# Half-precision queries and keys, shifted scan rows, and softmax blocks between stick-breaking blocks

## The chip, the core and the metric

One NeuronCore of a Trainium2 chip runs the whole layer in one launch. The metric is the device time in microseconds (us) of one execution. The engines are TensorE (PE, with its weight loads PEld), VectorE (DVE), ScalarE (ACT), GpSimd (POOL) and SyncE (SP), which here issues the DMAs.

## The reference

One layer on 2048 tokens of width 1024, all in float32:

```python
h = rmsnorm(x, attn_norm_w[l]); proj = h @ w_in[l]        # 1024 -> 3*256 + 3*512 + 3*256
(q_a, k_a, v_a, q_b, k_b, v_b, g_b, g_c, x_c) = jnp.split(proj, split_points, axis=-1)
y_sb = stick_breaking_attention(q_a, k_a, v_a)            # 4 heads of 64
# z = q.k/8;  w[t,s] = sigmoid(z_ts) * prod_{s<j<t} (1 - sigmoid(z_tj)), s < t
qh = rmsnorm(q_b, q_norm_w); kh = rmsnorm(k_b, k_norm_w)
y_ch = chunked_relpos_attention(qh, kh, v_b, rel_bias)    # 8 heads: softmax over a 576-key band + bias
y_cv = g_b * causal_depthwise_conv3(g_c * x_c)
x = x + group_rmsnorm(concat(y_sb, y_ch, y_cv)) @ w_out[l]
x = x + swiglu(rmsnorm(x, ffn_norm_w[l]), w_gate[l], w_up[l], w_down[l])   # d_ff 2816
```

The tokens come to the chip in reverse order, so "nearest keys first" runs along rising columns.

## The kernel before

Every projection takes each operand as a high and a low fp16 part and does three products (`mm3`). Queries and keys are kept as a high and a low part in fp32r (a float32 form that PE takes): `put_parts` writes both parts to DRAM (`kd`, `qd`), and `attend` loads a head's keys as one tile `K` (high part on partitions 0 to 63, low part on 64 to 127) and its queries twice, as `q1` (high, low) and `q2` (low, high). `scores` then needs two products for all four cross terms. A score tile of one block of 128 keys is computed 256 wide (`lead`).

Attention works on tiles of 128 queries. A *stick piece* has up to four blocks of 128 keys. Its `front` computes scores, on ACT two sigmoids (of z into `be`, of -z into `re`), and on DVE a running product of `re` (L609), the product of `be` with the row shifted by one column (L614), and, where an earlier piece of the same tile hands on a carry, a one-column product for column 0 (L612). `re` is a tile for one piece, two buffers. A *softmax piece* (`chunk_tile`) has up to five blocks: scores plus bias with a row maximum on DVE (L646), the negated maximum (L650), Exp with row sum on ACT (L652). In both kinds `mid` transposes the weights on PE, ACT scales and copies them to fp16 (L550), DVE takes the low part (L551); `back` multiplies by the values, and `put_y` writes the result.

The tokens are done in two halves, eight tiles of 128 each; the first half's pieces have few key blocks for the stick heads (1 to 8 a tile), the second's many (9 to 16). `weave` writes PE's order by hand: it takes piece after piece from `attend`, heads 0 to 3 (stick) and then 4 to 11 (softmax), and issues at each step `mid` of the piece three before, `back` of the piece five before and `front` of this one, with a stretch of other PE work between them. That other work is `fill`: the projections of both halves and the first half's output projection. Its steps have costs that add up in `clock` (0.65 for three 512-wide products, 0.33 for three 256-wide ones). How much of it goes between pieces is set by a pace: `origin + at * step - 0.5 * blocks` is what the clock should show after `at` pieces. A head may begin when its projections are `done`, which `later` sets some clock units after them; until then `run` issues fill alone:

```python
for head in range(12):
    need = (half, head // 2 if head < 4 else 2 + (head - 4) // 2)
    while need not in done:
        run(clock[0] + 0.5)
    for p in attend(half, groups, head):
```

On the other engines a planner orders the instructions by the program's order and by when it expects their inputs; each engine then runs its list in order. After the attention and the output projection the FFN of the first half, the second half's output projection and its FFN follow.

Of the kernel before, what the change touches and what calls it, by code (L numbers as in the profile page):

```python
# [9 lines left out]
F32 = mybir.dt.float32  # L10
# [12 lines left out]
NEG = -1e30  # L23
WSC = float(2 ** 14)
# [15 lines left out]
def trunk(ctx: ExitStack, tc: tile.TileContext, x, anw, w_in, qnw, knw, biasx, conv_w, onw, w_out,  # L40
# [18 lines left out]
    xp = ctx.enter_context(tc.tile_pool(name="xp", bufs=6))  # L59
# [12 lines left out]
    nc.gpsimd.affine_select(out=never, in_=never, pattern=[[1, 128]], compare_op=ALU.is_gt, fill=NEG,  # L72
# [4 lines left out]
    cw = consts.tile([128, 2, 3], F32, name="cw")  # L77
    halo = consts.tile([128, 2, 2], F32, name="halo")
# [245 lines left out]
    kd, qd = [{(p, i, j): dp.tile([128, HT], F32R, name=f"{n}d{p}_{i}{j}")  # L324
# [8 lines left out]
    def late_consts():  # L333
        for i, w in enumerate((qnw, knw)):
            for s in range(2):
                nc.sync.dma_start(nw[s * 64:(s + 1) * 64, i:i + 1], w.rearrange("(p o) -> p o", o=1))
        nc.vector.tensor_scalar(nw[:, 0:1], nw[:, 0:1], HD ** -0.5, None, op0=ALU.mult)
        for b in range(2):
            nc.sync.dma_start(cw[:, b, :], conv_w[:, b * 128:(b + 1) * 128].rearrange("t p -> p t"))
# [83 lines left out]
    def put_parts(src, pair, g, d, scale):  # L423

        half, c = where(g)
        hi = ap.tile([128, 520], F32R, name="sth", tag="w2")[:, :GRP]
        lo = ap.tile([128, 520], F32R, name="stl", tag="w2")[:, :GRP]
        nc.scalar.activation(hi, src, AF.Copy, scale=scale)
        nc.vector.scalar_tensor_tensor(lo, src, scale, f32(hi), op0=ALU.mult, op1=ALU.subtract)
        for part, st in enumerate((hi, lo)):  # L430
            nc.sync.dma_start(f32(d[pair, half, part][:, c:c + GRP]), f32(st))
# [23 lines left out]
    def stick_qk(H, groups, W, pair):  # L455
        key = ("qk", pair)
        u = W.get(key)
        for i, d in enumerate((kd, qd)):
            yield from proj_T(H, groups, u[i], lambda g, o, i=i, d=d: put_parts(o, pair, g, d, descale(key, i)))
# [117 lines left out]
    def scores(Q, cols, K, k0, n, diagonal=False):  # L577
# [3 lines left out]
        lead = 128 if n == 128 else 0  # L581
        kc = K[:, k0 - lead:k0 + n]
        nc.tensor.matmul(z[:, :n + lead], q1[:, cols], kc, start=True, stop=False)  # L583
        if diagonal:
            nc.tensor.matmul(z[:, lead:lead + 128], identb, never, start=False, stop=False)
        nc.tensor.matmul(z[:, :n + lead], q2[:, cols], kc, start=False, stop=True)
        return z[:, lead:lead + n]
# [4 lines left out]
    def stick_tile(T, head, K, k0, Q, V, cols):  # L592
# [3 lines left out]
        def piece(b, n):  # L596
# [38 lines left out]
    def chunk_tile(T, head, K, k0, Q, V, cols, bias):  # L635
# [4 lines left out]
        def front():  # L640
# [27 lines left out]
    def attend(half, groups, head):  # L668
# [4 lines left out]
        K = ap.tile([128, HT + more], F32R, name="k", tag="k")  # L673
# [346 lines left out]
```

## Time and profile before

| | |
|---|---|
| median of 3 runs | 2723.12 us (2720.71 to 2726.09) |
| the profiled execution | 2721.8 us, span 2719.9 us, mean granted PE clock 0.978 |
| first half's attention | 99 to 552 us |
| second half's stick heads | 552 to 960 us |
| second half's softmax heads | 960 to 1165 us |
| FFN, with one more output projection | 1288 us to the end |

Busy time is the time in which an engine has an instruction in work. PE's matmuls overlap in their pipeline, so PE can be called busy while its starts are further apart than they could be; the distance between starts is the better measure of one matmul's price.

### The profile page before, as it was taken

The page shows a single profiled execution, that of the slowest core. Times are in us where ns is not written, and L with a number is a line of the kernel's source. Part 1 is how long each engine was busy: PE and PEld are TensorE (multiplying, and loading weights), DVE is VectorE, ACT ScalarE, POOL GpSimd, SP SyncE. Part 2 cuts the span into 40 slices and gives each one's busy share as a digit, 9 for nine tenths or more (in the row PEclk, how much of TensorE's full clock was granted, in tenths as well). Part 3 has the DMA queues.
Part 4 walks back from the last instruction along what each step waited for, and adds up shares of the span by engine and source line. Part 5 has one row for each costly group of instructions (what it writes and reads, how often), then busy time and mean ns, then how long its engine had stood idle before and what let it go on. Part 6 is the DMA issues. An engine that isn't in the chain of part 4 may idle for free.

```text
span 2719.9 us, 41796 instructions
## 1 busy us (share of the span) xinstructions
PE 2548.8 (94%) x16258; PEld 1719.7 (63%) x16258; DVE 1472.0 (54%) x3535; ACT 1046.1 (38%) x1994; POOL 358.3 (13%) x389
## 2 busy tenths in 40 slices
PE   5998979998799889879999999999999999999999
PEld 4477766766687578754555555556864555555556
DVE  6467777689999878853443444333352333322234
ACT  5565756555455677663333333321121111111110
POOL 1123331102212211021111111110000000000000
PEclk8999989999999999989999999999999999999999
DMA  7644546554332267664332223232661111111101
GB/s 246 192 139 131 164 140 201 171 167 134 128 120 72 88 177 200 200 223 141 101 101 93 93 93 101 78 101 104 229 210 47 47 47 47 59 58 47 47 24 62
DMA packets 245063, 327.82 MB, mean 121 GB/s; under 512 B 77184, under 2 KB 168320, under 8 KB 244864
## 3 DMA queue, kind: packets, MB, share of 16 engines
q1 hardware_dynamic: 244864, 325.14, 37.8%
q8 instruction: 128, 2.10, 0.3%
q14 instruction: 71, 0.58, 0.1%
HBM read 220.21 MB, written 104.86 MB: 120 GB/s over the span
## 4 chain that ended last, share of the span: by engine, by line
PE 38%; DMA 4%; issue 4%; DVE 2%; POOL 1%; ACT 1%; SPq 0%; POOLq 0%; DVEq 0%; ACTq 0%
PE acc L318 7%; PE acc L320 7%; PE acc L319 7%; PE sc L937 5%; PE sc L938 5%; PE sc L939 5%; POOL w L225 1%; DMA wr<-in_w_down 1%; DMA x1d<-xs 1%; DMA wr<-in_w_up 1%; PE sc L273 0%; DMA xf<-x1d 0%; DVE gl L923 0%; DVE x L941 0%; DVE wl L258 0%
## 5 line engine op out<-in xcount | busy, mean ns | idle before, releaser
L318 PE MATMUL acc<-hh,w 128*128 128x512 f16 x1728 | 657.5, 381 | 0.0
L319 PE MATMUL acc<-hl,w 128*128 128x512 f16 x1728 | 656.3, 380 | 0.0
L320 PE MATMUL acc<-hh,w 128*128 128x512 f16 x1728 | 656.1, 380 | 0.0
L919 DVE SCALAR_TENSOR_TENSOR sg<-acc,ds,sg 128x512 f32<-128x512 f32 x88 | 66.0, 750 | 615.3 <-PE acc L320 533.5
L318 PE MATMUL acc<-w,hh 128*128 128x256 f16 x1408 | 392.5, 279 | 5.5 <-ACT w L224 4.0
L319 PE MATMUL acc<-w,hh 128*128 128x256 f16 x1408 | 390.4, 277 | 1.8 <-POOL w L225 1.8
L320 PE MATMUL acc<-w,hl 128*128 128x256 f16 x1408 | 390.1, 277 | 1.3 <-DVE rry L102 1.3
L941 DVE TENSOR_TENSOR x<-sc,x 128x512 f32<-128x512 f32 x352 | 241.3, 690 | 200.5 <-PE sc L939 193.7
L320 PEld LDWEIGHTS <-w 128*128 128x128 f16 x1728 | 169.3, 98 | 204.9 <-issue 1.8
L318 PEld LDWEIGHTS <-w 128*128 128x128 f16 x1728 | 169.3, 98 | 192.3 <-issue 15.8
L937 PE MATMUL sc<-wh,gh 128*128 128x512 f32 x704 | 278.7, 396 | 4.5 <-DVE x L941 4.5
L319 PEld LDWEIGHTS <-w 128*128 128x128 f16 x1728 | 169.6, 98 | 175.1 <-issue 1.1
L939 PE MATMUL sc<-wh,gl 128*128 128x512 f32 x704 | 274.2, 390 | 0.0
L938 PE MATMUL sc<-wl,gh 128*128 128x512 f32 x704 | 274.2, 389 | 0.0
L225 POOL TENSOR_TENSOR w<-wr,w 128x1024 f16<-128x1024 f32 x76 | 163.4, 2170 | 579.1 <-ACT w L224 523.6
L551 DVE SCALAR_TENSOR_TENSOR wtl<-tp,wth 128x512 f16<-128x512 f32 (+3 forms) x384 | 200.0, 529 | 50.5 <-ACT wth L550 49.7
L609 DVE TENSOR_TENSOR_SCAN re<-re,zero 128x512 f32<-128x512 f32 (+3 forms) x160 | 185.8, 1161 | 48.6 <-ACT re L606 48.3
L550 ACT ACTIVATE wth<-tp 128x512 f16<-128x512 f32 (+3 forms) x384 | 175.5, 475 | 81.9 <-PE tp L548 79.0
L922 ACT CAST gh<-sg 128x512 fp32r<-128x512 f32 x88 | 54.3, 617 | 378.7 <-DVE sg L919 378.7
L583 PE MATMUL sc<-k,q 128*128 128x320 f32 (+3 forms) x384 | 161.8, 425 | 4.8 <-ACT re L606 1.8
L318 PEld LDWEIGHTS <-hh 128*128 128x128 f16 x1408 | 140.1, 100 | 41.1 <-issue 19.9
L223 ACT ACTIVATE wr<-wr,wsc 128x1024 f32<-128x1024 f32 x76 | 83.4, 1141 | 191.2 <-DVE wsc L214 191.1
(153 smaller groups left out, 3798.2 us busy)
## 6 DMA issues: line engine op xcount, KB each, us to landing
w<-wd SPq DMA_DIRECT2D x92, 512.0 KB, 4.2
wd<-w SPq DMA_DIRECT2D x76, 512.0 KB, 2.7
q<-qd SPq DMA_DIRECT2D x192, 128.0 KB, 2.9
wr<-in_w_down SPq DMA_DIRECT2D x44, 512.0 KB, 4.3
k<-kd SPq DMA_DIRECT2D x56, 256.0 KB, 4.0
wr<-in_w_gate SPq DMA_DIRECT2D x22, 512.0 KB, 4.8
wr<-in_w_up SPq DMA_DIRECT2D x22, 512.0 KB, 6.0
xt<-in_x SPq DMA_DIRECT2D x16, 512.0 KB, 5.6
```

The costliest lines, as they stand in the source:

```text
L225: nc.gpsimd.tensor_tensor(w[:, 1, :], raw, w[:, 0, :], ALU.subtract)
L318: nc.tensor.matmul(o, sh(k), mh(k), start=(k == 0), stop=False)
L319: nc.tensor.matmul(o, sh(k), ml(k), start=False, stop=False)
L320: nc.tensor.matmul(o, sl(k), mh(k), start=False, stop=(k == n - 1))
L550: nc.scalar.activation(wh[:, s], tp[:, c], AF.Copy, scale=WSC)
L551: nc.vector.scalar_tensor_tensor(wl[:, s], tp[:, c], WSC, wh[:, s], op0=ALU.mult, op1=ALU.subtract)
L583: nc.tensor.matmul(z[:, :n + lead], q1[:, cols], kc, start=True, stop=False)
L609: nc.vector.tensor_tensor_scan(re[:, :N], re[:, :N], zero.to_broadcast([128, N]), start, ALU.mult, ALU.add)
L937: nc.tensor.matmul(o, gh[:, cs], wh[:, cc], start=st, stop=False)
L938: nc.tensor.matmul(o, gh[:, cs], wl[:, cc], start=False, stop=False)
L939: nc.tensor.matmul(o, gl[:, cs], wh[:, cc], start=False, stop=en)
L941: nc.vector.tensor_tensor(x1, o, x1, ALU.add)
```

## The change

Queries and keys are stored as fp16 parts (both scaled by a power of two: `DOWN` for the stick heads, a scale from the norm weights for the softmax heads), and the scales are undone in the sigmoids, the maximum and the Exp by operands from memory (`ZS`, `qks`); the bias is multiplied by the same scale on POOL. `lead` goes. The row `re` becomes one tile for all pieces of a query tile, with a 1 written ahead of its first column, so that the shifted product covers column 0 as well. In the second half, from the second stick head on, each stick tile is followed by two softmax tiles. Buffer counts change.

```diff
-    xp = ctx.enter_context(tc.tile_pool(name="xp", bufs=6))
+    xp = ctx.enter_context(tc.tile_pool(name="xp", bufs=5))
-    kd, qd = [{(p, i, j): dp.tile([128, HT], F32R, name=f"{n}d{p}_{i}{j}")
+    kd, qd = [{(p, i, j): dp.tile([128, HT], F16, name=f"{n}d{p}_{i}{j}")
 # late_consts: two more loads of the norm weights, their maxima, a power of two from each
+        nc.vector.tensor_tensor(nw, nw, m, ALU.mult)
+        nc.vector.tensor_tensor(qks[:, 0:1], m[:, 0:1], m[:, 1:2], ALU.mult)
+        nc.vector.reciprocal(qks[:, 1:2], qks[:, 0:1])
+        nc.vector.tensor_scalar(qks[:, 2:3], qks[:, 1:2], -1.0, None, op0=ALU.mult)
 # put_parts
-        hi = ap.tile([128, 520], F32R, name="sth", tag="w2")[:, :GRP]
-        lo = ap.tile([128, 520], F32R, name="stl", tag="w2")[:, :GRP]
-        nc.scalar.activation(hi, src, AF.Copy, scale=scale)
-        nc.vector.scalar_tensor_tensor(lo, src, scale, f32(hi), op0=ALU.mult, op1=ALU.subtract)
+        st = ap.tile([128, 2, 520], F16, name="st", tag="w2")[:, :, :GRP]
+        nc.scalar.activation(st[:, 0, :], src, AF.Copy, scale=scale)
+        nc.vector.scalar_tensor_tensor(st[:, 1, :], src, scale, st[:, 0, :], op0=ALU.mult, op1=ALU.subtract)
 # stick_qk
-            ... put_parts(o, pair, g, d, descale(key, i)))
+            ... put_parts(o, pair, g, d, DOWN))
 # scores
-        lead = 128 if n == 128 else 0
-        kc = K[:, k0 - lead:k0 + n]
+        kc = K[:, k0:k0 + n]
 # stick_tile, front
-                re = ap.tile([128, 512], F32, name="re", tag="re")
+                if b == T:
+                    state["re"] = ap.tile([128, NB * 128 + 8], F32, name="re", tag="re")
+                    nc.gpsimd.memset(state["re"][:, 0:1], 1.0)
+                e = state["re"][:, (b - T) * 128:(b - T) * 128 + N + 1]
+                re = e[:, 1:N + 1]
-                nc.scalar.activation(be[:, :N], z, AF.Sigmoid, scale=HD ** -0.5)
-                nc.scalar.activation(re[:, :N], z, AF.Sigmoid, scale=-HD ** -0.5)
-                carry = state.get("carry")
-                start = 1.0 if carry is None else carry
-                nc.vector.tensor_tensor_scan(re[:, :N], re[:, :N], zero.to_broadcast([128, N]), start,
-                                             ALU.mult, ALU.add)
-                if carry is not None:
-                    nc.vector.tensor_tensor(be[:, 0:1], be[:, 0:1], carry, ALU.mult)
-                state["carry"] = re[:, N - 1:N]
-                MUL.tensor_tensor(be[:, 1:N], be[:, 1:N], re[:, 0:N - 1], ALU.mult)
+                nc.scalar.activation(be[:, :N], z, AF.Sigmoid, scale=ZS[head // 2][:, 0:1])
+                nc.scalar.activation(re, z, AF.Sigmoid, scale=ZS[head // 2][:, 1:2])
+                nc.vector.tensor_tensor_scan(re, re, zero.to_broadcast([128, N]),
+                                             1.0 if b == T else e[:, 0:1], ALU.mult, ALU.add)
+                MUL.tensor_tensor(be[:, 0:N], be[:, 0:N], e[:, 0:N], ALU.mult)
 # chunk_tile, front
-            nc.vector.tensor_scalar(nm, m[:, 0:1], other, -1.0, op0=ALU.max, op1=ALU.mult)
+            nc.vector.tensor_scalar(nm, m[:, 0:1], other, qks[:, 2:3], op0=ALU.max, op1=ALU.mult)
-            nc.scalar.activation(s[:, :n * 128], s[:, :n * 128], AF.Exp, bias=nm, accum_out=tot)
+            nc.scalar.activation(s[:, :n * 128], s[:, :n * 128], AF.Exp, bias=nm, scale=qks[:, 1:2],
+                                 accum_out=tot)
 # attend: K, q1, q2 in F16; each tile's pieces are handed on as one list
+            nc.gpsimd.tensor_scalar(bias, bias, qks[:, 0:1], None, op0=ALU.mult)
 # weave
+        def tiles_of(half, groups, heads):
+            for head in heads:
+                need = (half, head // 2 if head < 4 else 2 + (head - 4) // 2)
+                while need not in done:
+                    run(clock[0] + 0.5)
+                yield from attend(half, groups, head)
+        def pieces_of(half, groups):
+            stick, chunk = (tiles_of(half, groups, h) for h in (range(4), range(4, 12)))
+            for n, tile in enumerate(stick):
+                yield from tile
+                if half == 1 and n >= 4 * len(groups):
+                    for tile in islice(chunk, 2):
+                        yield from tile
+            for tile in chunk:
+                yield from tile
+            for p in pieces_of(half, groups):
+                ...
-            BUFS = dict(k=2, q=4, be=5, re=2, w2=8, wth=3, wtl=3, v=2, vst=1, yu=2, bias=2)
+            BUFS = dict(k=3, q=8, be=5, re=2, w2=7, wth=3, wtl=3, v=3, vst=1, yu=2, bias=2)
```

## Rows read from the trace of the kernel before

**Rows 1.** The page: busy us, share and instructions of each engine.

```profile
PE 2548.8 (94%) x16258; PEld 1719.7 (63%) x16258; DVE 1472.0 (54%) x3535; ACT 1046.1 (38%) x1994; POOL 358.3 (13%) x389
```

**Rows 2.** Busy time by stage: length, each engine's busy us, granted clock, DMA.

```profile
99.00:302.00 203.00, 184.96 (x1503) 139.23 (x1501) 146.27 (x285) 124.66 (x254) 58.67 (x57) 0.96 0.49 144
302.00:552.00 250.00, 226.32 (x1900) 174.07 (x1898) 178.35 (x693) 151.92 (x366) 50.11 (x95) 0.97 0.57 168
552.00:640.00 88.00, 86.72 (x671) 57.63 (x669) 76.91 (x143) 55.13 (x113) 6.33 (x15) 1.00 0.46 143
640.00:762.00 122.00, 95.78 (x862) 77.72 (x860) 120.86 (x272) 56.82 (x116) 40.09 (x28) 0.94 0.41 132
762.00:856.00 94.00, 88.96 (x867) 75.27 (x865) 84.66 (x160) 54.26 (x109) 18.56 (x21) 1.00 0.31 94
856.00:960.00 104.00, 93.84 (x716) 66.55 (x716) 90.88 (x171) 64.81 (x122) 21.96 (x19) 0.92 0.32 106
960.00:1165.00 205.00, 183.88 (x1899) 165.54 (x1898) 165.56 (x656) 147.36 (x360) 29.69 (x78) 0.98 0.65 184
...
1288.00:2720.00 1432.00, 1415.20 (x6871) 861.44 (x6869) 511.65 (x885) 280.97 (x395) 88.48 (x41) 1.00 0.26 85
```

**Rows 3.** Timeline of PE's matmuls at four places.

```profile
708.01 0.36 PE L583 MATMUL sc<-k,q 128*128 128x256 f32 x1
...
708.34 0.28 PE L318 MATMUL acc<-w,hh 128*128 128x256 f16 x1
...
804.61 0.47 PE L583 MATMUL sc<-k,q 128*128 128x512 f32 x1
...
805.16 0.28 PE L318 MATMUL acc<-w,hh 128*128 128x256 f16 x1
...
1064.01 0.39 PE L583 MATMUL sc<-k,q 128*128 128x320 f32 x1
...
1064.67 0.28 PE L318 MATMUL acc<-w,hh 128*128 128x256 f16 x1
...
1182.60 0.38 PE L318 MATMUL acc<-hh,w 128*128 128x512 f16 x1
...
1182.82 0.38 PE L319 MATMUL acc<-hl,w 128*128 128x512 f16 x1
```

**Rows 4.** DMA issues: count, KB each, us to landing.

```profile
k<-kd SPq DMA_DIRECT2D x56, 256.0 KB, 4.0
```

**Rows 5.** DVE's groups, 552 to 960: busy us, mean ns, idle before, releaser.

```profile
L609 DVE TENSOR_TENSOR_SCAN re<-re,zero 128x512 f32<-128x512 f32 (+2 forms) x111 | 132.2, 1191 | 19.7 <-ACT re L606 19.6
L614 DVE TENSOR_TENSOR be<-be,re 128x511 f32<-128x511 f32 (+2 forms) x111 | 81.7, 736 | 0.6
L551 DVE SCALAR_TENSOR_TENSOR wtl<-tp,wth 128x512 f16<-128x512 f32 (+2 forms) x113 | 68.8, 609 | 0.3 <-ACT wth L550 0.2
L612 DVE TENSOR_TENSOR be<-be,re 128x1 f32<-128x1 f32 x80 | 18.6, 233 | 8.4 <-ACT be L605 8.1
```

**Rows 6.** ACT's groups, 552 to 960.

```profile
L606 ACT ACTIVATE re<-sc 128x512 f32<-128x512 f32 (+2 forms) x112 | 61.6, 550 | 41.9 <-DVE re L609 26.2 <-DVE be L612 15.3
```

**Rows 7.** POOL's groups by shape, 0 to 1400.

```profile
L470 POOL TENSOR_TENSOR qs<-qk 128x512 f32<-128x512 f32 x32 | 35.5, 1108 | 65.0 <-ACT qk L468 64.5 <-POOL bias L688 0.4
```

**Rows 8.** ACT's groups by shape, 0 to 1300.

```profile
L468 ACT ACTIVATE qk<-acc,ds 128x512 f32<-128x512 f32 x32 | 22.0, 689 | 4.5 <-PE acc L320 4.5
...
L446 ACT ACTIVATE vst<-acc 128x512 f16<-128x512 f32 x24 | 14.4, 601 | 15.9 <-PE acc L320 8.1 <-DMA vd<-vst 4.7 <-DMA xt<-in_x 0.7
```

**Rows 9.** DVE's groups, 960 to 1165.

```profile
L650 DVE TENSOR_SCALAR nm<-m 128x1 f32<-128x1 f32 x64 | 13.4, 210 | 0.7
...
L106 DVE TENSOR_SCALAR rrt<-rry,sa 128x1 f32<-128x1 f32 x12 | 3.2, 268 | 0.2
```

**Rows 10.** Timeline of ACT at a border of stages: start us, us, instruction.

```profile
551.28 1.28 ACT L605 ACT_TABLE_LOAD   x1
552.58 0.60 ACT L605 ACTIVATE be<-sc 128x512 f32<-128x512 f32 x1
```

More of the change, by code (lines that the diff above doesn't have):

```diff
@@ L23 @@
 NEG = -1e30
+NEVER = -1e37
 WSC = float(2 ** 14)
@@ L71, in trunk @@
     nc.vector.memset(never, 0.0)
[L72 removed]
+    nc.gpsimd.affine_select(out=never, in_=never, pattern=[[1, 128]], compare_op=ALU.is_gt, fill=NEVER,
                             base=0, channel_multiplier=-1)
@@ L77, in trunk @@
     cw = consts.tile([128, 2, 3], F32, name="cw")
+    qks = consts.tile([128, 3], F32, name="qks")
     halo = consts.tile([128, 2, 2], F32, name="halo")
@@ L425, in put_parts @@
         half, c = where(g)
-        hi = ap.tile([128, 520], F32R, name="sth", tag="w2")[:, :GRP]
-        lo = ap.tile([128, 520], F32R, name="stl", tag="w2")[:, :GRP]
-        nc.scalar.activation(hi, src, AF.Copy, scale=scale)
-        nc.vector.scalar_tensor_tensor(lo, src, scale, f32(hi), op0=ALU.mult, op1=ALU.subtract)
-        for part, st in enumerate((hi, lo)):
-            nc.sync.dma_start(f32(d[pair, half, part][:, c:c + GRP]), f32(st))
+        st = ap.tile([128, 2, 520], F16, name="st", tag="w2")[:, :, :GRP]
+        nc.scalar.activation(st[:, 0, :], src, AF.Copy, scale=scale)
+        nc.vector.scalar_tensor_tensor(st[:, 1, :], src, scale, st[:, 0, :], op0=ALU.mult, op1=ALU.subtract)
+        for part in range(2):
+            nc.sync.dma_start(d[pair, half, part][:, c:c + GRP], st[:, part, :])
     def v_block(H, groups, W, c0, head0, prep=None):
@@ L457, in stick_qk @@
         u = W.get(key)
+        if pair not in ZS:
+            zs = consts.tile([128, 2], F32, name=f"zs{pair}")
+            nc.vector.tensor_tensor(zs[:, 0:1], descale(key, 0), descale(key, 1), ALU.mult)
+            nc.vector.tensor_scalar(zs[:, 0:1], zs[:, 0:1], HD ** -0.5 / DOWN ** 2, 1e-30, op0=ALU.mult,
+                                    op1=ALU.max)
+            nc.vector.tensor_scalar(zs[:, 1:2], zs[:, 0:1], -1.0, None, op0=ALU.mult)
+            ZS[pair] = zs
         for i, d in enumerate((kd, qd)):
-            yield from proj_T(H, groups, u[i], lambda g, o, i=i, d=d: put_parts(o, pair, g, d, descale(key, i)))
+            yield from proj_T(H, groups, u[i], lambda g, o, i=i, d=d: put_parts(o, pair, g, d, DOWN))
     def chunk_qk(H, groups, W, pair):
@@ L672, in attend @@
         more = 0 if half == 0 else (HT if stick else 512)
-        K = ap.tile([128, HT + more], F32R, name="k", tag="k")
+        K = ap.tile([128, HT + more], F16, name="k", tag="k")
         V = ap.tile([128, (HT + more) // 128, 2, HD], F16, name="v", tag="v")
@@ L677, in attend @@
             at = slice(j * 64, j * 64 + 64)
-            nc.sync.dma_start(f32(K[at, :HT]), f32(kd[head // 2, half, j][rows, :]))
+            nc.sync.dma_start(K[at, :HT], kd[head // 2, half, j][rows, :])
             if more:
-                nc.sync.dma_start(f32(K[at, HT:]), f32(kd[head // 2, 0, j][rows, :more]))
+                nc.sync.dma_start(K[at, HT:], kd[head // 2, 0, j][rows, :more])
         nc.sync.dma_start(V[:, :HT // 128], vd[head // 4 * 4, half][:, :, head % 4])
@@ L690, in attend @@
             c = where(g)[1]
-            q1 = ap.tile([128, GRP], F32R, name="q1", tag="q")
-            q2 = ap.tile([128, GRP], F32R, name="q2", tag="q")
+            q1 = ap.tile([128, GRP], F16, name="q1", tag="q")
+            q2 = ap.tile([128, GRP], F16, name="q2", tag="q")
             for j in range(2):
-                src = f32(qd[head // 2, half, j][rows, c:c + GRP])
+                src = qd[head // 2, half, j][rows, c:c + GRP]
                 for i, q in enumerate((q1, q2)):
                     at = (i + j) % 2 * 64
-                    nc.sync.dma_start(f32(q[at:at + 64, :]), src)
+                    nc.sync.dma_start(q[at:at + 64, :], src)
             for t in range(3, -1, -1):
@@ L701, in attend @@
                 if stick:
-                    yield from stick_tile(T, head, K, k0, (q1, q2), V, cols)
+                    yield list(stick_tile(T, head, K, k0, (q1, q2), V, cols))
                 else:
-                    yield from chunk_tile(T, head, K, k0, (q1, q2), V, cols, bias)
+                    yield list(chunk_tile(T, head, K, k0, (q1, q2), V, cols, bias))
     def y_norm(T, gain, tmp):
@@ L866, in weave @@
             at = 0
-            for head in range(12):
-                need = (half, head // 2 if head < 4 else 2 + (head - 4) // 2)
-                while need not in done:
-                    run(clock[0] + 0.5)
-                for p in attend(half, groups, head):
-                    if origin is None:
-                        origin = clock[0]
-                        step = (ends[half] - origin + BLK * blocks) / pieces
-                    at += 1
-                    spent += BLK * p[3]
-                    gap = max(0.0, origin + at * step - spent - clock[0])
-                    line.append(p)
-                    stage(i, gap)
-                    i += 1
+            for p in pieces_of(half, groups):
+                if origin is None:
+                    origin = clock[0]
+                    step = (ends[half] - origin + BLK * blocks) / pieces
+                at += 1
+                spent += BLK * p[3]
+                gap = max(0.0, origin + at * step - spent - clock[0])
+                line.append(p)
+                stage(i, gap)
+                i += 1
         for _ in range(LAG2):
```

22 lines of the change are left out of this document (18 added, 4 removed).

## The prediction

> **What bounds the kernel now.** I read the busy times first, then a table of busy time by stage, then the groups of instructions of the stage that the change reorders, then single instructions. The page's busy times [rows 1] name TensorE (PE), 94%; as an average this misleads. The table by stage [rows 2] shows why: from 1288 us on, the FFN keeps PE 99% busy, and no edit touches it. The change lives before that. There the second half of the tokens runs its stick-breaking heads from 552 to 960 us and its softmax heads from 960 to 1165, and the two stretches have different limits. In the first, VectorE (DVE) is busy 373.3 of 408 us (91.5%), and from 640 to 762 even 120.9 of 122, with PE at 79% and a granted clock of 0.94. In the second, DVE is at 81%, PE at 90%. Over both: DVE 538.9, PE 549, ScalarE (ACT) 378.4 of 613 us. So the plan to mix the two kinds of blocks aims at real slack, but at most 613 - 539 = 74 us of it, less what the mixing costs. The first half (99 to 552 us) keeps its order; PE is busy 411 of 453 us there.
>
> **Half-precision queries and keys.** Two products per piece of scores. A 512-wide fp32 pair took 805.16 - 804.61 = 0.55 us from its first start to the next instruction; a 512-wide fp16 product elsewhere starts 0.22 us after the one before it, so the pair becomes 0.43: 0.12 less [rows 3]. The four 320-wide products of a softmax block took 0.66 us; at 0.22 x 320/512 each, 0.54: also 0.12. A one-block piece, computed today 256 wide, took 0.33; 128 wide it would be 0.11: 0.22 less. By the code's loops there are 112 four-block stick pieces (24 of them in the first half), 16 each of one, two and three blocks, 96 five-block softmax pieces (32 in the first half) and 8 each of the four shorter kinds. Taking 0.11 for two and three blocks, the first half saves 14.9 us and the second 20.6 us of PE time. In the first half PE is 91% busy, but partly in waits for buffers that DVE frees; I take 8 us of the 14.9 (bounds 0 and 15). In the second half it counts where PE is the limit: in head 0's stretch (552 to 640, PE 99%), 28 pieces, about 4 us.
>
> The halved transfers of queries and keys cost nothing and, I think, give nothing: loads of keys land in 4.0 us [rows 4] and are issued a head ahead. The staging buffers shrink from 8 to 7 and the row buffers from 6 to 5; I price this at 0 to 5 us, and take 0, since two staging tiles became one.
>
> **Shifted scan rows.** They remove the one-column multiply: 80 times 233 ns in the second half, 18.6 us of DVE [rows 5]. They also give each tile its own long row, where before two short buffers made ACT wait 41.5 us for DVE [rows 6]; DVE in its turn waited 19.6 + 8.1 us for ACT [rows 5]. Added are 64 one-column memsets on POOL, which has room (from 552 to 1165 at most a third busy in any stretch [rows 2]), and 16 multiplies of the bias by a scalar; nearest row 1.1 us for a 512-wide two-input product [rows 7], behind a load that POOL waits for already. Behind them in POOL's queue stand the output adds, which nothing near needs. I take 0 (bounds 0 and 8).
>
> **Scalars from memory.** Sigmoid scales and the Exp scale become per-partition operands. On ACT such an operand costs 689 - 601 = 0.088 us [rows 8]: 224 sigmoids and 64 Exps in the second half, 25 us of ACT. On DVE the nearest rows are 268 ns for two such operands against 210 for one [rows 9]: 64 x 0.058 = 3.7 us. DVE in the second half: 538.9 - 18.6 + 3.7 = 524.
>
> **The new order.** Each stick tile from head 1 on (24 of them) is followed by two softmax blocks; 16 softmax blocks remain for the end. Two things follow that the diff doesn't say.
>
> First, the pacing. `weave` keeps a clock of projection work (a unit is about a us of PE) and refuses a head until its projections are done. The second half starts at 8 units past its first query/key pair. Up to the first softmax head's permission stand the second pair (20.8), convolution (31.2), values (21.1), softmax pair 0 (21.1) and a delay of 20, so 106 units after the start. The pace's step comes out at (599.8 - 316.6 + 0.5 x 720 blocks) / 176 pieces = 3.65, so when the first softmax head is asked for, after 31 pieces with 109 blocks, the clock stands at 31 x 3.65 - 54.5 = 59. So 47 units of projections are issued in one lump with no attention between them, and the following 29 or so pieces get none, until the pace catches up. In the lump PE is full and DVE nearly idle: outside the attention lines DVE does 373.3 - 301.3 = 72 us over the stage's 210 units [rows 2, 5], so 16 us here, with three pieces in flight 23 of 47. This is the loss that the mixing has to earn back.
>
> Second, ACT's function tables. Sigmoid and Exp don't share one: at the border between softmax and stick stretches stands a table load of 1283 ns, and 1.30 us from its start the Sigmoid follows [rows 10]. Today's order pays this at each border. The new one pays it twice per tile-and-two-blocks round, 48 times, and up to 96 times if the planner's order lets the next tile's Sigmoid in between two Exps.
>
> **The sum for the second half.** Head 0: 88 - 4 = 84 us (DVE 72). The lump: 47 (DVE 23). The last 16 softmax blocks at 205/64 us: 51 (DVE 41). A wait for the first softmax head's keys, which are written just before: 4 (one load [rows 4]; bounds 0 and 8). Left for the 24 rounds is 524 - 72 - 23 - 41 = 388 us of DVE. ACT in them: 378.4 + 25, less 60 in head 0, 20 in the lump and 37 at the end, so 286 plus 48 x 1.3 = 349. PE: 549 - 20.6 - 84 - 47 - 46 = 351. So DVE stays the limit, ACT close behind. How dense can DVE be? From below, 81% as in today's softmax stretch; from above 99% as from 640 to 762. I take 93%, a little over the stage's own 91.5%, for the shorter ACT waits, and not more, for ACT at 349 of the rounds' time is far busier than its 231 of 408 in the stick stretch. 388 / 0.93 = 417. Total 84 + 47 + 51 + 4 + 417 = 603 against 613: 10 us less. With 8 us from the first half: 18 us. The profiled execution took 2721.8 us (span 2719.9), so 2704; the median of the runs shown stands 1.3 above it, so **2705**.
>
> **Rivals.**
> *Dense rounds.* DVE reaches 99% in the rounds: 392 instead of 417, and the first half gives its full 15: 2705 - 25 - 7 = 2673. For it: DVE did this for 122 us on end. Against: ACT was then busy 47% [rows 2].
>
> *Table loads on the path: slower.* ACT runs in order. While it loads a table, the copies of transposed weights behind the load stand, DVE's subtraction waits for them, and PE's next transposes wait for DVE (two PSUM buffers). If the 48 loads are felt in full, 48 x 1.3 = 62 us: 2767. It decides from 18 / 1.3 = 14 felt loads on. With 96 loads ACT would need 286 + 125 = 411 us in the rounds and be itself the limit. For it: DVE waited for ACT even at ACT's low load [rows 5]. Against: three pieces lie between scores and transposes, some 9 us of slack. The Trainium skill ("ScalarE: Activation LUTs", sections "What ACT_TABLE_LOAD costs" and "Table sets: the hidden batching unit") speaks against this order: it says to batch calls by table set, and gives a switch 1283 ns plus a drain of about 1380 ns, 2.66 us. The row agrees with the load and shows no such drain: the next Sigmoid starts 1.30 us after the load's start. By the page's figure the 48 loads would cost an estimated 128 us, and this rival would end at 2833.
>
> *Nothing comes of it.* PE's and DVE's savings fall in stretches that another engine limits, the lump eats what the mixing gives: 2722. For it: both engines near 88% over the half, so neither edit alone moves a clear limit. Against: DVE at 99% for a stretch, from which 18.6 us of work go.
>
> **Chances.** Forecast (2690 to 2717) 0.45, dense 0.15, loads on the path 0.28, nothing 0.12. Against the median, 0.2% (5.4 us) is about what a measurement of this kernel tells from no change. Faster: 0.43 of the forecast, all of dense, 0.02 of the rest, 0.60. Within: 0.02 + 0.09 + 0.04, 0.15. Slower: 0.25. The range runs from 2665, just under dense, to 2755, where two thirds of the loads are felt; beyond it lie the full loads.
>
> **What would show it.** The lump: some 47 us in which PE runs projections alone with DVE half idle, starting three pieces into head 1, then a stretch of about 75 us without projections, PE about half busy, its granted clock at or below 0.94. The loads: ACT table loads from 6 to between 50 and 100, 1.28 us each. DVE: no one-column multiply; first-half stretch shorter by about 8 us; the second half's attention over by 1140 to 1155 us. Score products at fp16 start 0.22 us apart at 512 columns. I am wrong on the mechanism if DVE's busy share in the rounds is under 85% with waits on ACT behind the loads (then slower), or if the lump isn't there.

## The result, and the profile after

The changed kernel takes **2794.67 us** (median of 4 runs, 2793.59 to 2797.55) against 2721.91 for the kernel before on the same chip: ratio **1.0274, 95% interval [1.0261, 1.0287]**, slower by some 73 us. The forecast was 2705, the range 2665 to 2755: the sign is wrong, and the time lies outside the range, beyond the price that the one rival pointing this way got from rows (2767).

The page after, busy time of each engine; it answers to [rows 1].

```profile
PE 2568.3 (92%) x16258; PEld 1703.8 (61%) x16258; DVE 1458.4 (52%) x3455; ACT 1142.5 (41%) x2040; POOL 395.0 (14%) x469
```

DVE has 80 instructions and 14 us less. ACT gained 46 instructions and 96 us, PE 20 us with the same 16258 instructions. Busy time by stage after, columns as in [rows 2]:

```profile
99.00:300.00 201.00, 179.03 (x1517) 136.02 (x1516) 142.84 (x271) 133.13 (x255) 61.38 (x89) 0.97 0.40 120
300.00:551.00 251.00, 222.03 (x1897) 166.52 (x1895) 184.54 (x691) 156.63 (x364) 63.88 (x104) 0.97 0.45 132
551.00:637.00 86.00, 84.37 (x668) 54.81 (x667) 74.74 (x126) 59.48 (x116) 10.24 (x21) 1.00 0.33 101
637.00:717.00 80.00, 65.14 (x569) 54.73 (x566) 60.89 (x184) 19.51 (x34) 33.30 (x24) 0.94 0.52 174
717.00:803.00 86.00, 53.02 (x447) 38.39 (x447) 60.22 (x151) 67.29 (x124) 10.29 (x23) 0.84 0.20 52
803.00:1011.00 208.00, 177.57 (x1574) 134.76 (x1573) 158.52 (x395) 149.00 (x267) 42.78 (x67) 0.96 0.20 59
1011.00:1174.00 163.00, 135.09 (x1200) 108.44 (x1199) 120.22 (x292) 127.41 (x231) 28.91 (x40) 0.90 0.50 155
1174.00:1227.00 53.00, 50.27 (x536) 43.74 (x534) 44.87 (x168) 39.01 (x92) 7.35 (x19) 1.00 0.29 82
1288.00:2793.00 1505.00, 1490.46 (x7165) 891.47 (x7163) 529.93 (x925) 301.40 (x425) 95.38 (x44) 1.00 0.26 87
```

The first half ends at 551.0 us (552.6 before [rows 10]). From 637 to 717 stands the lump of projections, ACT busy a quarter of the time. From 717 the mixed rounds run; in their first 86 us PE is busy 62% at a granted clock of 0.84 (the trace has the clock at full or at half speed, and the rows give the mean over a stretch). Over all rounds (717 to 1174) DVE is busy 339.0 of 457 us, 74%, and ACT 343.7, 75%. The attention ends at 1227 instead of 1165.

One border of a round, 717 to 725 us (start, duration, instruction, idle time before it and its releaser):

```profile
716.60 1.28 ACT L676 ACT_TABLE_LOAD   x1
717.89 0.92 ACT L676 ACTIVATE s<-s,nm,qks 128x640 f32<-128x640 f32 x1
...
718.81 0.91 ACT L676 ACTIVATE s<-s,nm,qks 128x640 f32<-128x640 f32 x1
718.96 0.77 PE L574 MATMUL tp<-ident,s 128*128 128x128 f32 x5 [1.75 <-ACT s L676]
...
719.83 1.28 ACT L634 ACT_TABLE_LOAD   x1
...
721.12 0.69 ACT L634 ACTIVATE be<-sc,zs 128x512 f32<-128x512 f32 x1
721.71 0.68 ACT L635 ACTIVATE re<-sc,zs 128x512 f32<-128x512 f32 x1
722.28 0.76 ACT L576 ACTIVATE wth<-tp 128x384 f16<-128x384 f32 x2
722.42 1.23 DVE L636 TENSOR_TENSOR_SCAN re<-re,zero 128x512 f32<-128x512 f32 x1 [2.22 <-ACT re L635]
...
723.56 0.53 DVE L577 SCALAR_TENSOR_TENSOR wtl<-tp,wth 128x384 f16<-128x384 f32 x1
...
724.15 1.62 PE L574 MATMUL tp<-ident,s 128*128 128x128 f32 x5 [3.66 <-DVE wtl L577]
```

Both Exps of a round stand between one pair of loads, so a round pays two, not four. From the first load's start to the Sigmoid ACT spends 4.5 us. Behind it DVE's scan waits 2.22 us for the Sigmoid. ACT's copies of transposed weights (`wth`) come only after both Sigmoids, DVE's subtraction (`wtl`) after them, and PE's transposes, whose PSUM buffer that subtraction frees, wait 3.66 us. From the groups of the rounds (717 to 1180), ACT's table loads, then DVE's 512-wide scans (busy us, mean ns, idle before, releaser):

```profile
L676 ACT ACT_TABLE_LOAD x24 | 30.8, 1283 | 0.4
L634 ACT ACT_TABLE_LOAD x23 | 29.5, 1283 | 0.4
```

```profile
L636 DVE TENSOR_TENSOR_SCAN re<-re,zero 128x512 f32<-128x512 f32 x64 | 81.3, 1270 | 62.8 <-ACT re L635 62.6
```

### The profile page after: what moved, and what is told of

Its sections match the earlier page's. It is cut to its first block, busy times and chain, and to the rows that moved or that the text cites. A ratio compares the mean times of both kernels' runs of the same rounds, so it can differ in the third digit from the quotient of the medians.

```text
span 2793.7 us, 41910 instructions
## 1 busy us (share of the span) xinstructions
PE 2568.3 (92%) x16258; PEld 1703.8 (61%) x16258; DVE 1458.4 (52%) x3455; ACT 1142.5 (41%) x2040; POOL 395.0 (14%) x469
## 5 line engine op out<-in xcount | busy, mean ns | idle before, releaser
L577 DVE SCALAR_TENSOR_TENSOR wtl<-tp,wth 128x384 f16<-128x384 f32 (+3 forms) x384 | 201.3, 530 | 42.3 <-ACT wth L576 40.5
L576 ACT ACTIVATE wth<-tp 128x384 f16<-128x384 f32 (+3 forms) x384 | 176.0, 476 | 84.1 <-PE tp L574 82.9
L574 PE MATMUL tp<-ident,s 128*128 128x128 f32 x560 | 98.5, 294 | 76.7 <-DVE wtl L577 54.8
```

Source lines behind the costliest of these rows:

```text
L574: nc.tensor.transpose(tp[:, (b - b0) * 128:(b - b0 + 1) * 128], src[:, b * 128:(b + 1) * 128], ident)
L576: nc.scalar.activation(wh[:, s], tp[:, c], AF.Copy, scale=WSC)
L577: nc.vector.scalar_tensor_tensor(wl[:, s], tp[:, c], WSC, wh[:, s], op0=ALU.mult, op1=ALU.subtract)
```

## Theories and experiments

The loss stands in the second half's attention, apart from some 10 us in the FFN. Two theories for the attention: the **loads** (each stops ACT for 1.3 us, and DVE and PE behind it), or the **order** itself (the lump, the rounds short of projections behind it, or mixing as such). Against both: the other edits (fp16, shifted rows). In e2, e6, e7, e12, e14 and e15 Sigmoid stands in place of Exp, so these kernels leave out the softmax's exponential. "Padding" is 896 bytes left free ahead of the FFN's buffers; its section says why.

| | what | median us | ratio to before, 95% | head 1 to the FFN's first gate, us | table loads |
|---|---|---|---|---|---|
| before | | 2719 to 2722 | | 550 | 6 |
| after | | 2794.67 | [1.0261, 1.0287] | 618 | 52 |
| e1 | old order | 2718.85 | [0.9977, 1.0003] | 544 | 6 |
| e2 | no loads | 2754.62 | [1.0098, 1.0142] | 577 | 3 |
| e4 | eight blocks after four tiles | 2743.62 | [1.0064, 1.0096] | 567 | 18 |
| e5 | after + padding (one run) | 2781.3 | – | 614 | 52 |
| e6 | no loads, from head 2, three a tile | 2728.05 | [1.0013, 1.0036] | 549 | 3 |
| e7 | e2, pace set anew | 2757.22 | [1.0130, 1.0166] | 581 | 3 |
| e8 | e1 + padding | 2707.89 | [0.9935, 0.9967] | 541 | 6 |
| e9 | fp16 alone + padding | 2708.84 | [0.9939, 0.9966] | 545 | 6 |
| e10 | e1 with loads put in | 2745.03 | [1.0048, 1.0097] | 566 | 54 |
| e11 | e6 with Exp | 2746.71 | [1.0086, 1.0118] | 571 | 36 |
| e12 | e2, softmax projections earlier | 2748.04 | [1.0087, 1.0121] | 571 | 3 |
| e13 | before + padding (one run) | 2733.85 | – | 550 | 6 |
| e14 | e2, one block a tile | 2741.98 | [1.0068, 1.0098] | 564 | 3 |
| e15 | e12, one block a tile | 2743.23 | [1.0072, 1.0106] | 562 | 3 |

The last two columns are of one trace each: e2's is of the longest of its four runs (2749.9 to 2760.5), e15's of the shortest (2737.7 to 2745.2). By the intervals a difference between two rows is known to some 4 to 8 us.

### Undo the order (e1)

```diff
-            for n, tile in enumerate(stick): ...
+            for tile in tiles_of(half, groups, range(12)):
+                yield from tile
```

> The changed kernel with only the order undone: stick heads first, then softmax heads; fp16 queries and keys, shifted rows and buffer counts stay. Changed kernel: 2794.7 us, second half's attention 551 to 1227 us. Whatever in the new order costs the time (table loads, the lump of projections, or the mixing itself), it must come back here: table loads 6 again, second half's attention 595 to 615 us long, total 2705 to 2730. If the total stays above 2760, the cost is in the other edits and all theories of the order fall.

2718.85 us: all the loss, 75.8 us, is the order's. The other edits together, as they stand, can't be told from no change; most of why, the padding shows below.

### No loads, same order (e2)

```diff
-            nc.scalar.activation(s..., AF.Exp, bias=nm, scale=qks[:, 1:2], ...)
+            nc.scalar.activation(s..., AF.Sigmoid, bias=nm, scale=qks[:, 1:2], ...)
```

> The changed kernel with Sigmoid in place of Exp in the softmax blocks (the weights are wrong by that; every instruction keeps its place and size), so that no table is changed in the rounds. Theory of the felt loads: 46 loads of 1.3 us go, 60 us or more back, total 2735 or less. Theory of the lump (projections issued in one piece, then rounds without any): the lump is still there, at most ACT's own time is seen, total 2775 to 2795. Theory of the mixing itself (a softmax block takes both transpose buffers, the lag of three pieces is short): likewise 2775 to 2795.

2754.62: 40.1 us of the 75.8 come back. The loads fall from 52 to 3. DVE's 512-wide scans in the rounds (722 to 1138), and busy times over the rounds in three stretches:

```profile
L636 DVE TENSOR_TENSOR_SCAN re<-re,zero 128x512 f32<-128x512 f32 x63 | 79.4, 1260 | 27.8 <-ACT re L635 27.8
```

```profile
722.00:808.00 86.00, 64.16 (x602) 49.29 (x603) 77.05 (x195) 62.46 (x137) 13.16 (x30) 0.92 0.22 58
808.00:1015.00 207.00, 178.11 (x1585) 135.31 (x1584) 156.83 (x392) 132.66 (x264) 47.01 (x69) 0.96 0.27 80
1015.00:1138.00 123.00, 107.35 (x1035) 89.56 (x1036) 101.01 (x248) 87.34 (x175) 20.27 (x32) 0.96 0.53 166
```

Their wait for ACT's Sigmoid is 27.8 instead of 62.6 us (scans of all widths: 38.1 instead of 69.5), a fall of nearly the size of the gain. Per load (49) 0.82 us of 1.30 is felt. The other 35.7 us of the order remain with hardly a load left.

### Loads in the old order (e10)

The order is undone as in e1, and (other lines left out):

```diff
+                    if T < NB // 2 and head >= 1:   # 24 tiles: re's first column = exp(0)
+                        nc.scalar.activation(state["re"][:, 0:1], zero, AF.Exp)
+                    else:
                         nc.gpsimd.memset(state["re"][:, 0:1], 1.0)
```

> Heads in order with both edits, no pad (2718.9 us), and 48 added table loads: for the 24 tiles of the second, third and fourth stick head of the second half the 1 ahead of the row is written by an Exp of a zero column on ACT instead of a memset on POOL. No mixing, no lump. Felt loads: 46 loads cost 40 us when they were taken out of the new order, so 48 here cost some 42 us, total about 2760. If a load costs only where it stands behind a softmax block (mixing): under 10 us, 2720 to 2728.

ACT at one such tile:

```profile
697.13 1.28 ACT L631 ACT_TABLE_LOAD   x1
698.43 0.20 ACT L631 ACTIVATE re<-zero 128x1 f32<-128x1 f32 x1
698.64 1.28 ACT L637 ACT_TABLE_LOAD   x1
699.93 0.69 ACT L637 ACTIVATE be<-sc,zs 128x512 f32<-128x512 f32 x1
```

2745.03, 26.2 us over e1 for 48 loads: 0.55 us each. So loads cost in an order without lump or mixing as well, at less than half their length. The 24 Exps themselves, 0.20 us of ACT each, are in this sum.

### Fewer loads: eight blocks after every four tiles (e4)

```diff
-                if half == 1 and n >= 4 * len(groups):
-                    for tile in islice(chunk, 2):
+                if half == 1 and n >= 4 * len(groups) and n % 4 == 3:
+                    for tile in islice(chunk, 8):
```

> The changed kernel with coarser rounds: eight softmax tiles after every fourth stick tile, from the second stick head on. Loads in the rounds 12 instead of 48. Felt loads: 36 x 1.3 = 47 us back, total about 2748. Lump: the first softmax head is asked for three stick tiles later, the lump falls from 47 units to about 26, 20 to 25 us back, about 2772. Mixing itself: two kinds of pieces meet at 12 places instead of 48, the total near that of the heads in order, 2705 to 2730.

2743.62 with 18 loads: 51 us under the changed kernel, though only 34 loads fewer. At 0.82 each that is 28. The rest came with the coarser mixing or with the smaller lump (47 us between two score products instead of 69); this run doesn't separate them.

### Begin at head 2 (e6, and e11 with Exp)

```diff
-                if half == 1 and n >= 4 * len(groups):
-                    for tile in islice(chunk, 2):
+                if half == 1 and n >= 8 * len(groups):
+                    for tile in islice(chunk, 3):
```

> As the kernel with Sigmoid for Exp (2754.6 us, second half's attention 637 us), but the softmax tiles start with the third stick head, three after each stick tile: by the code's clock the projections are then done and no lump is issued. Heads in order took 603 us for the second half's attention, 2718.9 in all, so 34 us of the new order are not table loads. Theory of the lump and of the rounds without projections: nearly all of the 34 us come back, total 2715 to 2728. Theory of the mixing itself: with three softmax tiles a round the mixing is as fine, the total stays at 2745 to 2760.

> The changed kernel with Exp, the softmax tiles starting with the third stick head, three after each stick tile: 32 loads in the rounds, no lump. With Sigmoid the same order took 2728.1 us. If each load costs what 46 cost in the new order (40 us, 0.87 each): 2728 + 28 = 2756. If a load costs what it did with the heads in order (26 us for 48, 0.54 each): 2745. If loads only hurt together with the lump: below 2735.

Without loads 2728.05, 26.6 us under e2 with as many blocks mixed (48), three a tile, but begun a head later; 9.2 over the old order. With Exp 2746.71: 18.7 us for 33 loads, 0.57 each, as in e10. So the early start, with all that goes with it, costs the most after the loads. That a load costs more behind such a start (0.82 against 0.57) is what the two differences say, but they lie close to what the runs can tell apart. Was it the lump?

### The lump: pace set anew (e7), projections earlier (e12), one block a tile (e14, e15)

e7 sets the pace anew after the lump, so that no rounds without projections follow (the lines that count the pieces left are left out):

```diff
-                if origin is None:
+                if origin is None or clock[0] - last > 20.0:
```

> As the kernel with Sigmoid for Exp in the new order (2754.6 us), but after the lump the pace is set anew over the pieces that are left, so that no rounds go without projections; the lump itself stays. Starting with the third head took away lump and starved rounds together and gave 26.6 us. If the starved rounds are the cost: 2730 to 2735. If the lump itself is (80 us for some 47 us of projections and three pieces): 2750 to 2756. Shared: about 2742.

2757.22, as e2: in the 88 us behind the lump PE is now busy 76.4 (64.2 of 86 in e2), but DVE only 69.4 (77.1 in e2), and nothing is gained. e12 takes the lump away at its cause (the order of the weights' loads changes with it):

```diff
+            if half == 1:
+                yield from v_block(H[half], groups, W, C_VB, 4)
+                yield from chunk_qk(H[half], groups, W, 0)
+                later(20.0, lambda: done.add((1, 2)))
             yield from stick_qk(H[half], groups, W, 1)
```

> The new order from head 1 on with two softmax blocks a tile, Sigmoid in place of Exp (so no loads), and in the second half the values and queries and keys of the first two softmax heads projected ahead of the second pair of stick heads. By the planner's clock these heads are then ready 62 units after the start, where they are asked for at 59, so that hardly any lump is left there; some 20 units remain later, where the third softmax head is asked for at 114 and ready at 135. If the lump is what the order costs beside the loads, the 26.6 us between the same order with a lump (2754.6) and the start at head 2 (2728.1) come back but for about a third: 2728 to 2740. If the cost is the early start with two blocks a tile itself, the time stays at 2750 to 2757.

2748.04: the first softmax activation starts 12 us after head 1 (81 in e2), and the longest pause between two score products is 14.5 us (69 in e2), so the lump is gone, but only 6.6 us come back; the expectation had left a second shortage open. e14 and e15 are e2 and e12 with `islice(chunk, 1)`; e15 should have no shortage anywhere.

> The new order from head 1 on, Sigmoid in place of Exp, with one softmax block after each stick tile instead of two (24 mixed, 40 at the end). The lump of projections at the start of head 1 stays. If lumps are the cost: 2745 to 2755, as with two blocks (2754.6). If the early start of the mixing is: half as much of it, so some 14 us less, 2736 to 2744.

> As the run before it, with the first two softmax heads' projections ahead of the second pair of stick heads. By the planner's clock no head is then asked for before it is ready (head 1: 62 against 59; the third softmax head after 100 pieces at 161 against 135), so no lump is left anywhere. If lumps are the cost: 2722 to 2732, some 25 us under the run before it. If the early start is: within 7 us of the run before it.

2741.98 and 2743.23: the same, though e14 has the lump and e15's longest pause is 11.6 us. The theory that the lump is what the order costs falls. Taking it away isn't free, for the earlier projections lengthen head 0 from 86 to 91 and 92 us (e12, e15); but from head 1 to the gate, too, it gives only 6 and 2 us of the 26.6. The early mixing costs less when it is half as dense: 12.6 us less with the lump; the 4.8 without it are about what the runs can tell. Much of where it is lost the first 150 us of head 1 show. Busy times in them for e1, e6, e15, e12, e14, e2 and the changed kernel, in this order (for e1 and the changed kernel also from there to the FFN's first gate):

```profile
633.00:783.00 150.00, 121.72 (x1156) 101.24 (x1154) 144.60 (x297) 80.35 (x149) 49.19 (x45) 0.97 0.35 116
783.00:1177.00 394.00, 353.95 (x3381) 285.99 (x3379) 319.55 (x919) 275.50 (x575) 90.00 (x137) 0.97 0.39 117
```

```profile
635.00:785.00 150.00, 122.15 (x1154) 100.52 (x1153) 143.97 (x317) 80.66 (x154) 50.30 (x47) 0.97 0.35 115
```

```profile
636.00:786.00 150.00, 126.54 (x1019) 90.50 (x1018) 133.68 (x309) 82.33 (x164) 28.02 (x38) 0.90 0.29 92
```

```profile
641.00:791.00 150.00, 126.31 (x1038) 91.30 (x1037) 131.86 (x346) 84.37 (x175) 34.20 (x44) 0.92 0.31 96
```

```profile
639.00:789.00 150.00, 112.56 (x1001) 89.87 (x999) 126.44 (x324) 71.54 (x142) 42.20 (x45) 0.92 0.35 113
```

```profile
641.00:791.00 150.00, 114.97 (x1017) 91.46 (x1016) 122.28 (x337) 72.38 (x150) 41.45 (x48) 0.92 0.39 122
```

```profile
637.00:787.00 150.00, 105.73 (x904) 83.92 (x901) 108.78 (x305) 74.82 (x135) 42.17 (x43) 0.89 0.37 116
787.00:1255.00 468.00, 400.51 (x3632) 314.89 (x3633) 347.05 (x911) 343.79 (x636) 90.33 (x139) 0.94 0.34 102
```

Third engine column, DVE: head 1 in the old order keeps it 96% busy and is thus the one stretch with nothing to fill. Begun there, the mixing leaves DVE idle 16, 18, 24 and 28 us of the 150 (e15, e12, e14, e2; 6 in e6), and from head 1 to the gate these kernels take 13 to 28 us longer than e6. That both go together is read from the rows; e12 and e14 stand in the other order on the second count (22 and 15 us longer), so it is not the whole account. The granted clock of the stretch is 0.90 to 0.92 instead of 0.97, lowest in e15, where DVE idles least. In e15 and e12 PE is busy 126 us instead of 122, but its products cover no more columns than in e1 (242 thousand against 245): it does the same work in more busy time, at the lower clock, while DVE does 11 to 13 us less. What DVE waits for differs: where the lump is (e2, e14) mostly for POOL's squares of softmax queries and keys (13.4 and 15.8 us), where it is not (e15, e12) mostly for ACT's Sigmoid (8.3 and 8.5 us; 3.8 in e1). No run takes one of these waits away by itself, so why the early start costs what it does stays open in part.

PE's part of the loss: from head 1 to the gate it is busy 506.2 us in the changed kernel and 475.7 in e1, for 4536 and 4535 instructions of the same work, 30.5 us of the 74; the idle time makes up 43.5. The granted clock over these 618 and 544 us is 0.93 and 0.97, which goes with the longer busy time.

### The padding (e5, e13, e8)

Beyond the attention the FFN lost time too, with none of its code changed. In the changed kernel its down products start 0.23 us apart and more:

```profile
1959.80 0.39 PE L978 MATMUL sc<-wh,gh 128*128 128x512 f32 x1
1960.03 0.39 PE L979 MATMUL sc<-wl,gh 128*128 128x512 f32 x1
1960.27 0.39 PE L980 MATMUL sc<-wh,gl 128*128 128x512 f32 x1
1960.49 0.39 PE L978 MATMUL sc<-wh,gh 128*128 128x512 f32 x1
...
1961.20 0.40 PE L978 MATMUL sc<-wh,gh 128*128 128x512 f32 x1
```

Six intervals in 1.40 us are 233 ns; the median over all is 232, before 227. There are 2112 of them: 5 ns each make 10.6 us. In the built programs the first buffers of the two operands `wh` and `gh` lie 76,800 bytes apart before, a multiple of 1024, and 72,832 after (their other buffers are whole multiples of 2048 bytes further on). 896 bytes ahead of `gh` make it 73,728, a multiple again:

```diff
+    pad = fp.tile([128, 224], F32, name="pad")
+    nc.gpsimd.memset(pad[:, 0:1], 0.0)
```

> The changed kernel with 896 bytes per partition left free ahead of the FFN's buffers, nothing else. In the trace of the changed kernel the FFN's last products (fp32, 512 wide) start 232 ns apart, before 227, and 2112 of them make 10 us; nothing in the FFN was edited, but buffer addresses moved. If the distance between the two operands' addresses (a multiple of 1024 bytes before, 128 bytes off after, a multiple of 1024 again with the pad) sets it, the products start 227 ns apart again and the total is 10 us less, 2784. If it is something else, 232 ns and 2795.

> The kernel before with the same 896 bytes left free ahead of the FFN's buffers: here they move the two operands' distance off a multiple of 1024 bytes. If that distance sets the start distance of the FFN's last products, they go from 227 to 232 ns and the FFN gets some 10 us longer, 2732. If the pad helps by something else, 227 ns and 2722.

One of the three products over the whole FFN (busy us, mean ns), in the kernel before, in the changed kernel, in the changed kernel with the padding (e5), and in the kernel before with the padding, which takes it off the multiple (e13):

```profile
L937 PE MATMUL sc<-wh,gh 128*128 128x512 f32 x704 | 278.7, 396 | 4.5 <-DVE x L941 4.5
```

```profile
L978 PE MATMUL sc<-wh,gh 128*128 128x512 f32 x704 | 282.0, 401 | 2.4 <-DVE x L982 2.2
```

```profile
L980 PE MATMUL sc<-wh,gh 128*128 128x512 f32 x704 | 278.2, 396 | 2.1 <-DVE x L984 2.1
```

```profile
L939 PE MATMUL sc<-wh,gh 128*128 128x512 f32 x704 | 282.2, 401 | 2.8 <-DVE x L943 2.7
```

The median spacing is 227, 232, 227 and 232 ns, and the times follow: 2781.3 in e5 (13 less than the changed kernel), and 2733.85 in e13 (13 more than the 2720.6 of before). Both are single runs, but e8, the median of six, says the same: 11 us under e1.

> Heads in order, with fp16 and shifted rows, and the 896 bytes ahead of the FFN's buffers. The pad's look moved the FFN's last products back from 232 to 227 ns and shortened the FFN part by 13 us. Expected 2718.9 less 11 to 13: 2706 to 2708, faster than before by about 0.5%. If the pad's gain was chance: 2719.

**2707.89 us, 0.9951 [0.9935, 0.9967]**: the old order with fp16, shifted rows and the padding beats both kernels.

### Fp16 alone (e9)

The old row code (`re` per piece, the one-column product) with fp16, the scalars from memory and buffer counts that came with it, the old order and the padding.

> The same without the shifted rows: short row buffers, carry and one-column product as before; so fp16 queries and keys alone, heads in order, with the pad. The prediction gave fp16 12 us (8 in the first half, 4 in the second) and the rows some 18 us of DVE work in the second half. If so: 2710. If DVE was the limit wherever PE was relieved: 2718 to 2724, and the shifted rows carry all of the difference to the kernel with both.

2708.84: fp16, with what came with it, is worth 12 to 13 us against the kernel before, whose operands lie on the multiple too, and the shifted rows 1, less than the runs can tell. In head 1, DVE's scan and shifted product over 120 us of e8, then the shifted and the one-column product of e9:

```profile
L636 DVE TENSOR_TENSOR_SCAN re<-re,zero 128x512 f32<-128x512 f32 x24 | 31.8, 1324 | 0.0
L638 DVE TENSOR_TENSOR be<-be,re 128x512 f32<-128x512 f32 x24 | 25.5, 1061 | 0.0
```

```profile
L639 DVE TENSOR_TENSOR be<-be,re 128x511 f32<-128x511 f32 x23 | 20.5, 891 | 0.0
L637 DVE TENSOR_TENSOR be<-be,re 128x1 f32<-128x1 f32 x21 | 6.1, 290 | 0.0
```

The one-column products go, 6.1 us here, but the shifted product takes 1061 ns instead of 891 in the mean: 24 x 0.17 = 4.1 us come back. The added column is not the cause. In e8 15 of the 24 take 0.67 to 0.69 us, as 18 of the 23 in e9. Each of the others overlaps a product of two inputs on POOL and ends some 0.55 us after it, as this one in e8 does (start, duration):

```profile
641.62 3.14 POOL L745 TENSOR_TENSOR yt<-yt,gain 128x1024 f32<-128x1024 f32 x1 [1.36 <-DVE yt L744]
...
643.11 2.19 DVE L638 TENSOR_TENSOR be<-be,re 128x512 f32<-128x512 f32 x1
```

There are nine such in e8 and five in e9, so the 4.1 us are these meetings; whether the longer row brings them about was not tried. Outside head 1 DVE isn't the limit, so what the rows save there was hidden.

## Why the prediction was wrong

The second half, term by term (predicted, then measured from the first score of head 0 at 551.0 us): head 0 84, 86; lump and key wait 51, 80 (these 80 hold three pieces that the prediction had in its rounds); rounds 417, 457; last 16 blocks 51, 53; sum 603, 676. The first half gave 1.6 us instead of 8, and the FFN lost 10 that no term held: 2704 + 73 + 6 + 10 = 2793, and the profiled execution took 2795.5.

- **The step that failed: "I take 93%".** DVE's density in the rounds was worked out from the stretches where DVE alone was busy, although the same paragraph had ACT at 349 us of 417; the waits behind a table load had no term in the sum. With the loads the rounds reach 74%, under the 85% that the prediction named as the sign against its mechanism. Without them they reach 81% (e2: 77.05 + 156.83 + 101.01 = 334.9 of 416 us), which was the lower bound, the density of the old softmax stretch. DVE's work in the second half was right (524 predicted, 519.5 measured), but the rounds held 339 of it, not 388, for 61 instead of 23 fell into the lump's stretch. So it is luck that e2's rounds take 416 us, the forecast's 417: less work at less density. What failed under it was the premise that slack of different stages can be added: "real slack, but at most 74 us" was an average over stages. Mixed from head 1 on, DVE's one full stretch was no longer full, and no later stretch made up for it.
- **Loads on the path: the rival held.** It decided from 14 felt loads; the chain that it named (ACT's copies, DVE's subtraction, PE's transposes) is that of the border above. 40 of its 62 us were felt, 0.82 us a load; the argument against it, "some 9 us of slack" in three pieces, was no cover. It had 0.28; but it alone would have ended at 2705 + 40 = 2745, inside the range (whose end, 2755, is four fifths of the loads by the prediction's own price, not two thirds). The Trainium skill ("ScalarE: Activation LUTs", "Table sets: the hidden batching unit") says to batch calls by set, and the runs agree in direction; by its price of a switch ("What ACT_TABLE_LOAD costs", 2.66 us) 49 loads would be an estimated 130 us, and 40 were measured.
- **The lump: there, but it lasts longer and is not the cause.** Its place (three pieces into head 1) and the starved rounds behind it (717 to 803, PE 62%) came as told. Without its three pieces it took 69 us instead of 47, and PE was not full in it: with them PE is busy 65.1 of 80 us, at a clock of 0.94, and DVE, which was to be half idle, 60.9. Yet taking it away (e12, e15) gave back 6.6 and -1.3 us: "the loss that the mixing has to earn back" was put in the wrong place. Nothing was earned in any variant: the best (e6) is 9 us behind the old order.
- **Fp16: right in sum, not in place.** 8 + 4 predicted, 12 to 13 measured (e9). The first half is 453 us long before and 445 to 456, in the median 451, in the fourteen traces that have the change: some 2 of the 8. The rest came after it (before: head 0 to gate 639 us, e9 633; from there to the end 1529 and 1525), but the last 4 us are no more than the ends of such traces differ by (1535 to 1540 where the FFN runs without padding). So that the sum came out is in part luck. The prediction's counts give 21.8 us of PE for the second half, not 20.6; nothing hung on it.
- **Shifted rows: 18.6 us counted, 1 measured.** They counted only if DVE was the limit all through; it is in head 1 alone, and there DVE's waits beside POOL took most of that back. Such waits were in DVE's busy time from the start, and the prediction read all of it as work: by the durations of the same instructions without POOL beside them, an estimated 70 us of DVE's busy time ahead of the FFN in the kernel before.
- **Small prices.** Load 1283 ns, next activation 1.30 us after its start, as told. The rows after, for the scalars from memory, and for POOL:

```profile
L674 DVE TENSOR_SCALAR nm<-m,qks 128x1 f32<-128x1 f32 x128 | 34.4, 269 | 1.8
L712 POOL TENSOR_SCALAR bias<-bias,qks 128x640 f32<-128x640 f32 x16 | 32.8, 2050 | 80.4 <-DMA bias<-in_rel_bias 63.3 <-DVE st L448 7.6 <-DVE nm L674 6.7
L634 ACT ACTIVATE be<-sc,zs 128x512 f32<-128x512 f32 x112 | 77.6, 693 | 41.5 <-PE sc L611 40.9
```

269 and 693 ns stand as predicted (268; the 512-wide Sigmoid's 599 before and 88 more for the operand [rows 8], 687); the bias product took 2050 ns instead of some 1.1 us, behind the load that POOL waits for; no wait for it shows on another engine.

The account of the 75.8 us between e1 and the changed kernel, as differences of runs: loads 40 (e2), the start in head 1 instead of head 2 with all that goes with it 27 (e6 against e2), mixing as such 9 (e6 against e1). The loads are shown by taking them out and by putting them in (e2, e10, e11). Of the 27 the runs show that neither the lump nor the starved rounds make them up, and that half the density brings back some 13 of them where the lump stays; the wait behind them stays open.

## What to carry to other kernels

Slack that a table by stage shows in two stages can be joined only if each stage's full engine stays full after the join: look first for the stretch that is already full, and be wary of starting there (here a start one head later was 27 us better). In-order engines pay for a table load with whoever waits behind it, so an order that alternates two function sets is priced by the waits behind the load, not by the spare time of the engine; 0.55 to 0.82 of each 1.30 us was felt here, though ACT was busy at most 78% of any stage of the changed kernel's second half of tokens. A mean duration can hold waits: look at single instructions before a longer mean is called more work. Time the edits of one change one by one: here a gain of 12 us and a loss of 11 from a buffer's address hid each other.

## What the runs showed of the hardware

The spacing of the 512-wide f32 products was 227 ns where the distance of the two operands' addresses in the program is a multiple of 1024 bytes and 232 where it is not, in four programs (before, after, and each with 896 bytes of padding). Other distances were not tried, so that the multiple is the rule is a guess; that the addresses decide is shown. It moves this kernel by 11 to 13 us, 0.4 to 0.5%, about as much as fp16 gave.

A 512-wide DVE product of two inputs took 0.68 us by itself and up to 2.6 us where a two-input product of POOL was already running: it ended some 0.55 us after POOL's, in all 14 cases in the 120 us of head 1 of e8 and e9. This is read from the traces; no run moved POOL's products away.
